# More buffers for the scaled q, k, v sums ahead of the short convolution in a hybrid encoder trunk

## Chip, cores, metric

The kernel runs on one core of one Trainium2 chip, as one launch. The metric is device time in microseconds, the median of several runs. Engines are named as in the profile: PE (TensorE matmuls), DVE (VectorE), ACT (ScalarE), POOL (GpSimd), SP (SyncE, which issues the weight loads).

## What is computed

A two-layer encoder on 256 tokens of width 1024, all in float32. Each layer is half a SwiGLU, a mixer, half a SwiGLU. The mixer has two branches that read one projection `h @ w_in`, and the change lies in the first:

```
gq, gk, gv, gz, gb, ga, c_q, c_kv, k_rope, gate_logits = split_cols(h @ w_in[l])
# branch A, gated DeltaNet
qkv = centred_short_conv(concat([q, k, v]), conv_w)     # depthwise, 5 taps along the sequence, zero edges, then SiLU
qh, kh, vh = l2norm(q), l2norm(k), v                    # 4 heads of 128
o = chunked gated delta rule, forwards + backwards      # decays, a triangular inverse, a state
# branch B, latent attention
q = rmsnorm(c_q) @ w_uq;  kv = rmsnorm(c_kv) @ w_ukv;  softmax attention, 8 heads
y = sigmoid(g_A) * (A @ P_A) + sigmoid(g_B) * (B @ P_B);  x = x + y @ w_out
```

## The kernel before

Every dense product is three matmuls in a reduced float32 format: weights and activations are split into a high and a low part. A weight tile arrives by DMA as `raw`, ACT casts it to `whi` (line 130), DVE subtracts to get `wlo` (line 131), and PE multiplies high by high, low by high and high by low (lines 148 to 150, helper `mm3`). There are three buffers each of `raw`, `whi` and `wlo`, so PE paces the casts, and PE waits whenever a cast or a subtraction comes late.

The tile framework's scheduler decides the order of instructions on each engine from data dependences, buffer reuse and priorities; each engine then works through its own list in order. PSUM sums use the tag `acc` with three buffers.

The mixer takes q, k and v as six groups of 256 channels, `qkv_group(0)` to `(5)`; groups 0 and 1 are q, 2 and 3 are k, 4 and 5 are v. The program calls them in the order 2, 3, 0, 1, then much later 4 and 5. A group is 48 matmuls into one `acc` buffer (line 557), then on DVE: scale by the norm's row `rb` out of PSUM into `pre` (line 565), a first tap into `cv` for each half (line 571), four more taps for each half (line 573), then ACT's tanh into `th` (line 577) and DVE's product into `qkT` or `vT` (line 578). `pre`, `cv` and `th` have one buffer each. POOL writes zeros into the two edge columns at each end of `pre` (lines 563 and 564), which lets every tap read 256 columns.

What stands around it, in the order of the text: the gates' decays (`gdn_decay`: POOL multiplies masks at line 743 and masks the exponentials at line 755, PE sums at line 744), lengths of k (`lengths(4)`: POOL squares `qkT` into a `cv` buffer at line 586, PE sums at 590, DVE turns and reads at 593 and 594, POOL takes the power at 598), the latent of the attention (`latent`, split at lines 115 and 116), the products with `w_ukv` (512 wide) and `w_uq` (384 wide) in `mla_dense(0)`, the z product, coefficients (`nk` at line 714), the chunk matrices `LA` (PE 763, DVE 767), `mla_dense(1)`, two gate products of 512 columns (`gate`, ACT tanh into the tag `gate`, which has six buffers), and the triangular inverse: `gdn_base` copies `LA` into place (ACT 793, DVE 791), POOL runs 30 small steps (lines 805 and 807), DVE and ACT bring the result into `XC` and `ZC` (810 to 816), and PE's first product on it is line 839.

Of the kernel before, what the change touches and what calls it, by code (L numbers as in the profile page):

```python
# [16 lines left out]
ALU = mybir.AluOpType  # L17
# [3 lines left out]
P = 128  # L21
D = 1024
S = 256
# [14 lines left out]
def encoder_trunk(ctx: ExitStack, tc: tile.TileContext, x, positions, norm_ffn1, ffn1_w_gate, ffn1_w_up,  # L38
# [4 lines left out]
    V, A, G, T = nc.vector, nc.scalar, nc.gpsimd, nc.tensor  # L43
# [8 lines left out]
    def acc():  # L52
        return psum.tile([P, 512], F32, tag="acc", name="acc", bufs=3)
# [4 lines left out]
    def gdp():  # L58
        return psum.tile([P, 512], F32, tag="gd", name="gd", bufs=2)
# [59 lines left out]
    def weights(src, nk, w, pool=wpool):  # L119

        raw = wpool.tile([P, 2048], F32, tag="raw", name="raw", bufs=3)
        nc.sync.dma_start(out=raw[:, :nk * w].rearrange("p (k c) -> p k c", c=w),
                          in_=src.rearrange("(k p) c -> p k c", p=P))
        per = 1024 // w
        res = []
        for k0 in range(0, nk, per):
            n = min(per, nk - k0)
            hi = pool.tile([P, 1024], F32R, tag="whi", name="whi", bufs=3)
            lo = pool.tile([P, 1024], F32R, tag="wlo", name="wlo", bufs=3)
            A.copy(out=hi[:, :n * w], in_=raw[:, k0 * w:(k0 + n) * w])  # L130
            V.tensor_tensor(out=lo[:, :n * w], in0=raw[:, k0 * w:(k0 + n) * w], in1=hi[:, :n * w].bitcast(F32),  # L131
                            op=ALU.subtract)
            for k in range(n):
                res.append((hi[:, k * w:(k + 1) * w], lo[:, k * w:(k + 1) * w]))
        return res
# [289 lines left out]
    def mixer(l, next_gain):  # L425
# [7 lines left out]
        with tc.tile_pool(name="mix", bufs=1) as mp:  # L433
            def t2(tag, bufs, shape=(P, NH, P)):
                return mp.tile(list(shape), F32, tag=tag, name=tag, bufs=bufs)
# [17 lines left out]
            rb = mp.tile([P, S], F32, name="rb")  # L453
# [92 lines left out]
            def qkv_group(grp):  # L546

                ps = acc()
                pc = ps.rearrange("p (c s) -> p c s", c=2)
                ws = weights(wl_[:, grp * 256:(grp + 1) * 256], NKC, 256)  # L550

                for c in range(2):
                    cc = slice(c * P, (c + 1) * P)
                    terms = [m for kc, (wh, wlo) in enumerate(ws)
                             for m in ((wh, xh[:, kc]), (wh, xl[:, kc]), (wlo, xh[:, kc]))]
                    for i, (w, a) in enumerate(terms[::-1] if c else terms):
                        T.matmul(pc[:, c].rearrange("p (t s) -> p t s", s=P), lhsT=w[:, cc], rhs=a, start=(i == 0),  # L557
                                 stop=(i == len(terms) - 1))
                if grp >= 4:
                    vT[grp - 4] = ysb[0][:, (grp - 4) * 512:(grp - 3) * 512].rearrange("p (c s) -> p c s", s=S)  # L560
                pre = t2("pre", 1, (P, 2, S + 4))
                cv = t2("cv", 1, (P, 2, S))
                G.memset(pre[:, :, 0:2], 0.0)  # L563
                G.memset(pre[:, :, S + 2:S + 4], 0.0)
                V.tensor_tensor(out=pre[:, :, 2:S + 2], in0=pc, in1=rb[:, None, :].to_broadcast([P, 2, S]), op=ALU.mult)  # L565
                for c in range(2):
                    ch = grp * 2 + c
                    for d in range(5):
                        wc = ccol[:, l * 60 + d * 12 + ch:l * 60 + d * 12 + ch + 1]
                        if d == 0:  # L570
                            V.tensor_scalar(out=cv[:, c], in0=pre[:, c, 0:S], scalar1=wc, scalar2=None, op0=ALU.mult)
                        else:
                            V.scalar_tensor_tensor(out=cv[:, c], in0=pre[:, c, d:d + S], scalar=wc, in1=cv[:, c],  # L573
                                                   op0=ALU.mult, op1=ALU.add)

                th = t2("th", 1, (P, 2, S))
                A.activation(out=th, in_=cv, func=AF.Tanh, scale=0.5)
                V.scalar_tensor_tensor(out=qkT[:, grp * 2:grp * 2 + 2, :] if grp < 4 else vT[grp - 4], in0=th, scalar=1.0,
                                       in1=cv, op0=ALU.add, op1=ALU.mult)

            def lengths(c0):

                pss = gdp()[:, :4 * NT * 32].rearrange("p (c t s) -> p c t s", c=4, t=NT)
                for c in (0, 2):
                    sq = t2("cv", 1, (P, 2, S))
                    G.tensor_tensor(out=sq, in0=qkT[:, c0 + c:c0 + c + 2, :], in1=qkT[:, c0 + c:c0 + c + 2, :], op=ALU.mult)
                    sv = sq.rearrange("p c (t g s) -> p g c t s", t=NT, g=4)
                    for g in range(4):

                        T.matmul(pss[g * 32:(g + 1) * 32, c:c + 2], lhsT=ones, rhs=sv[:, g], start=True, stop=True)  # L590
                rows = t2("rows", 1, (P, 2, 4 * NT * 32))
                A.copy(out=rows[:, 0], in_=pss.rearrange("p c t s -> p (c t s)"))
                V.transpose(out=rows[:, 1], in_=rows[:, 0])
                V.tensor_scalar(out=ssq[:, :, c0:c0 + 4],
                                in0=rows[:, 1].rearrange("p (c t s) -> p t c s", c=4, t=NT)[:, :, :, 0],
                                scalar1=4.0 * EPS, scalar2=None, op0=ALU.add)
                for t in range(NT):
                    G.tensor_tensor(out=rqk[:, t, c0:c0 + 4], in0=ssq[:, t, c0:c0 + 4], in1=neghalf[:, :4], op=ALU.pow)
# [407 lines left out]

            rstd_row()
            qkv_group(2)
            dense(xh, xl, NKC, wl_, C_BA, 400, ev_ba)
            qkv_group(3)  # L1010
            qkv_group(0)
            dense(xh, xl, NKC, wl_, C_KV, 288, ev_kv)
            gdn_scalars()
            gdn_decay(0)
            lengths(4)
            cqT = latent(cq, QL, 0, G_Q + 3 * l)
            qkv_group(1)
# [36 lines left out]
            at1(0)  # L1054
            sts[1] = gdn_first(1)
            lengths(0)
            gdn_second(0, sts[0])
            ga = [gate(C_G)]
# [60 lines left out]
```

## Time and profile before

| | |
|---|---|
| median of 3 runs | 1235.73 us (1235.57 to 1237.52) |
| the profiled execution | 1238.92 us, of which the profile's span is 1237.2 us |
| mean granted TensorE clock | 0.985 of full speed |
| busy | PE 1204.2 us, DVE 770.9 us, ACT 622.4 us, POOL 132.3 us |

Busy time is the sum of an engine's instructions with overlaps counted once. The two layers behave alike: the same lines wait for the same lines twice, some 611 us apart. A wait is put down to the instruction that released it. Times of the trace below are in microseconds from the start of the span, and those of layer 0.

### The profile page before, as it was taken

Reading aid. Unit: us, or ns where it says so; the run is one execution under the profiler, and the core shown is the slowest. Engines: PE = TensorE matmul, PEld = TensorE weight load, DVE = VectorE, ACT = ScalarE, POOL = GpSimd, SP = SyncE. Lnnn points to the kernel's source line nnn. Section 1 sums busy time; section 2 is a strip of 40 time slices with the busy share of each in tenths; the row PEclk is TensorE's granted clock in tenths of the full one; section 3 lists DMA queues with packets and bytes.
Section 4 is the critical chain, followed back from the end, with each engine's and each line's share of the span. In section 5 each row is a group of like instructions: output and inputs, shape, how many; then the busy total and the mean of one; then the engine's idle time right before and its main releaser. Section 6 shows DMA issues by size and latency. Waiting matters only on the chain.

```text
span 1237.2 us, 17605 instructions
## 1 busy us (share of the span) xinstructions
PE 1204.2 (97%) x7064; PEld 1016.9 (82%) x7064; DVE 770.9 (62%) x1125; ACT 622.4 (50%) x911; POOL 132.3 (11%) x238
## 2 busy tenths in 40 slices
PE   9999999899999999999999999997999999999997
PEld 6888889778778888888888888897778888888886
DVE  5665556986857665554555554588858676555554
ACT  6554445547455454444454453465455455544443
POOL 1000001454101000000000000015540000000010
PEclk9999999989899999999999999998998999999999
DMA  7564555445222555556555556553453135565552
GB/s 265 181 197 144 201 188 179 139 125 174 94 88 103 171 185 189 176 173 207 187 178 187 186 170 194 182 158 122 124 168 104 69 138 186 178 198 180 191 187 85
DMA packets 114576, 202.70 MB, mean 164 GB/s; under 512 B 4107, under 2 KB 30399, under 8 KB 114495
## 3 DMA queue, kind: packets, MB, share of 16 engines
q1 hardware_dynamic: 114031, 200.52, 49.9%
q8 instruction: 55, 0.90, 0.3%
q10 hardware_dynamic: 464, 1.06, 0.2%
q14 instruction: 26, 0.21, 0.1%
HBM read 200.52 MB, written 1.05 MB: 163 GB/s over the span
## 4 chain that ended last, share of the span: by engine, by line
PE 87%; DVE 5%; POOL 4%; ACT 2%; issue 2%; DMA 0%; POOLq 0%; SPq 0%; ACTq 0%
PE acc L148 24%; PE acc L149 24%; PE acc L150 24%; PE acc L557 4%; PE ms L198 2%; DVE wlo L131 2%; POOL t L807 1%; PE ms L665 1%; POOL bt L805 1%; PE gd L148 1%; PE gd L149 1%; PE gd L150 1%; PE gd L938 1%; DVE cv L573 1%; PE gd L763 1%
## 5 line engine op out<-in xcount | busy, mean ns | idle before, releaser
L131 DVE TENSOR_TENSOR wlo<-raw,whi 128x1024 fp32r<-128x1024 f32 (+3 forms) x388 | 470.4, 1215 | 368.4 <-ACT whi L130 365.9
L130 ACT CAST whi<-raw 128x1024 fp32r<-128x1024 f32 (+3 forms) x388 | 399.3, 1033 | 424.0 <-PE acc L150 384.1
L149 PE MATMUL acc<-wlo,xh 128*128 128x512 f32 (+3 forms) x968 | 360.6, 374 | 0.0
L150 PE MATMUL acc<-whi,xl 128*128 128x512 f32 (+3 forms) x968 | 357.4, 372 | 0.0
L148 PE MATMUL acc<-whi,xh 128*128 128x512 f32 (+3 forms) x968 | 344.8, 376 | 0.1
L149 PEld LDWEIGHTS acc<-wlo,xh 128*128 128x128 f32 x968 | 182.4, 188 | 29.5 <-issue 0.4
L148 PEld LDWEIGHTS acc<-whi,xh 128*128 128x128 f32 x968 | 181.5, 189 | 30.3 <-ACT xh L115 0.8
L150 PEld LDWEIGHTS acc<-whi,xl 128*128 128x128 f32 x968 | 182.1, 188 | 29.3
L149 PE MATMUL acc<-wlo,hh 128*128 128x512 f32 x352 | 137.4, 390 | 0.0
L150 PE MATMUL acc<-whi,hl 128*128 128x512 f32 x352 | 137.1, 390 | 0.0
L148 PE MATMUL acc<-whi,hh 128*128 128x512 f32 x352 | 127.3, 392 | 0.0
L150 PEld LDWEIGHTS acc<-whi,hl 128*128 128x128 f32 x352 | 66.1, 188 | 13.8
L148 PEld LDWEIGHTS acc<-whi,hh 128*128 128x128 f32 x352 | 66.1, 188 | 13.7
L149 PEld LDWEIGHTS acc<-wlo,hh 128*128 128x128 f32 x352 | 66.1, 188 | 13.3
L148 PE MATMUL acc<-whi,fr 128*128 128x512 f32 (+1 forms) x152 | 60.3, 403 | 9.1 <-DVE pre L565 7.9
L149 PE MATMUL acc<-wlo,fr 128*128 128x512 f32 (+1 forms) x152 | 59.9, 396 | 0.0
L150 PE MATMUL acc<-whi,fr 128*128 128x512 f32 (+1 forms) x152 | 57.5, 395 | 2.4 <-DVE fr L116 2.4
L557 PE MATMUL acc<-xl,whi 128*128 128x256 f32 x192 | 55.3, 288 | 0.0
L557 PE MATMUL acc<-xh,wlo 128*128 128x256 f32 x192 | 54.2, 292 | 1.0 <-DVE wlo L131 1.0
L557 PE MATMUL acc<-xh,whi 128*128 128x256 f32 x192 | 54.9, 289 | 0.0
L573 DVE SCALAR_TENSOR_TENSOR cv<-pre,ccol,cv 128x256 f32<-128x256 f32 x96 | 51.5, 569 | 0.1
L563 POOL MEMSET pre<- 128x4 f32 x12 | 1.2, 104 | 425.3 <-PE acc L150 341.0
(298 smaller groups left out, 1271.9 us busy)
## 6 DMA issues: line engine op xcount, KB each, us to landing
raw<-in_ffn_w_up_dram SPq DMA_DIRECT2D x40, 1024.0 KB, 5.1
raw<-in_ffn_w_down_dram SPq DMA_DIRECT2D x40, 1024.0 KB, 4.9
raw<-in_ffn_w_gate_dram SPq DMA_DIRECT2D x38, 1024.0 KB, 5.0
raw<-in_w_in_dram SPq DMA_DIRECT2D x32, 1024.0 KB, 5.0
raw<-in_w_out_dram SPq DMA_DIRECT2D x8, 1024.0 KB, 4.9
raw<-in_ffn_w_gate_dram SPq DMA_DIRECT2D x12, 512.0 KB, 3.7
raw<-in_ffn_w_up_dram SPq DMA_DIRECT2D x8, 512.0 KB, 3.7
raw<-in_ffn_w_down_dram SPq DMA_DIRECT2D x8, 512.0 KB, 3.3
```

Source lines behind the costliest of these rows:

```text
L130: A.copy(out=hi[:, :n * w], in_=raw[:, k0 * w:(k0 + n) * w])
L131: V.tensor_tensor(out=lo[:, :n * w], in0=raw[:, k0 * w:(k0 + n) * w], in1=hi[:, :n * w].bitcast(F32), op=ALU.subtract)
L148: T.matmul(ps[t][:, :n], lhsT=a1, rhs=w[0], start=start, stop=False)
L149: T.matmul(ps[t][:, :n], lhsT=a1, rhs=w[1], start=False, stop=False)
L150: T.matmul(ps[t][:, :n], lhsT=a2, rhs=w[0], start=False, stop=stop)
L198: T.transpose(out=pt[:, i * S + t * P:i * S + (t + 1) * P], in_=srcs[t][:, (j + i) * P:(j + i + 1) * P], identity=ident)
L557: T.matmul(pc[:, c].rearrange("p (t s) -> p t s", s=P), lhsT=w[:, cc], rhs=a, start=(i == 0), stop=(i == len(terms) - 1))
L573: V.scalar_tensor_tensor(out=cv[:, c], in0=pre[:, c, d:d + S], scalar=wc, in1=cv[:, c], op0=ALU.mult, op1=ALU.add)
L665: T.matmul(sc[:, t * S:(t + 1) * S], lhsT=qT[:, t * P:(t + 1) * P], rhs=kT, start=True, stop=True)
L763: T.matmul(pa[:, (h - hp) * 256:(h - hp + 1) * 256], lhsT=qkT[:, 4 + h, t * P:(t + 1) * P], rhs=qkT[:, h:h + 5:4, t * P:(t + 1) * P], star ...
L805: G.tensor_tensor(out=tv, in0=M[:, b + 1:16, b:b + 1].to_broadcast([P, na, nb]), in1=Y[:, b:b + 1, 0:nb].to_broadcast([P, na, nb]), op=ALU ...
L807: G.tensor_tensor(out=Y[:, b + 1:16, 0:nb], in0=Y[:, b + 1:16, 0:nb], in1=tv, op=ALU.add)
```

## The change

Groups 0 to 3 now scale into a buffer of the tag `gate`, whose six buffers the gates' tanh uses only later; groups 4 and 5 keep `pre` with one buffer. `cv` has two buffers. The scaling instruction (line 565) is emitted under a priority. The tanh is written over the scaled sums, so `th` is gone. The zero edges are gone: the centre tap comes first and writes all 256 columns, and the others touch only the 254 or 255 columns that exist. Lines behind the edit move down by one (573 becomes 574, 577 becomes 578, and so on).

```diff
-                pre = t2("pre", 1, (P, 2, S + 4))
-                cv = t2("cv", 1, (P, 2, S))
-                G.memset(pre[:, :, 0:2], 0.0)
-                G.memset(pre[:, :, S + 2:S + 4], 0.0)
-                V.tensor_tensor(out=pre[:, :, 2:S + 2], in0=pc, in1=rb[:, None, :].to_broadcast([P, 2, S]), op=ALU.mult)
+
+                pre = t2("gate", 6, (P, 2, S)) if grp < 4 else t2("pre", 1, (P, 2, S))
+                cv = t2("cv", 2, (P, 2, S))
+                with tc.high_priority(offset=150):
+                    V.tensor_tensor(out=pre, in0=pc, in1=rb[:, None, :].to_broadcast([P, 2, S]), op=ALU.mult)
                 for c in range(2):
                     ch = grp * 2 + c
-                    for d in range(5):
+                    for d in (2, 0, 1, 3, 4):
                         wc = ccol[:, l * 60 + d * 12 + ch:l * 60 + d * 12 + ch + 1]
-                        if d == 0:
-                            V.tensor_scalar(out=cv[:, c], in0=pre[:, c, 0:S], scalar1=wc, scalar2=None, op0=ALU.mult)
+                        if d == 2:
+                            V.tensor_scalar(out=cv[:, c], in0=pre[:, c], scalar1=wc, scalar2=None, op0=ALU.mult)
                         else:
-                            V.scalar_tensor_tensor(out=cv[:, c], in0=pre[:, c, d:d + S], scalar=wc, in1=cv[:, c],
+                            o, i = (slice(2 - d, S), slice(0, S + d - 2)) if d < 2 else (slice(0, S + 2 - d), slice(d - 2, S))
+                            V.scalar_tensor_tensor(out=cv[:, c, o], in0=pre[:, c, i], scalar=wc, in1=cv[:, c, o],
                                                    op0=ALU.mult, op1=ALU.add)
 
-                th = t2("th", 1, (P, 2, S))
+                th = pre
...
-                    sq = t2("cv", 1, (P, 2, S))
+                    sq = t2("cv", 2, (P, 2, S))
```

The scheduler orders the mixer anew around this. Three places of layer 0 follow; layer 1 has the same order at each of them.

Place one is DVE at the scaling of group 0. Before, its row (line 565) comes when all taps of group 3 are done, and its own taps start three rows later, behind a weight tile:

```order
L573 SCALAR_TENSOR_TENSOR cv<-pre,ccol,cv 128x256
L536 TENSOR_TENSOR glog<-glog,alog 128x16
L131 TENSOR_TENSOR wlo<-raw,whi 128x1024
L565 TENSOR_TENSOR pre<-acc,rb 128x2x256
L578 SCALAR_TENSOR_TENSOR qkT<-th,cv 128x512
L113 TENSOR_TENSOR gl<-glog,gh 128x16
L131 TENSOR_TENSOR wlo<-raw,whi 128x1024
L476 TENSOR_SCALAR krope<-acc,rstd 128x32
L571 TENSOR_SCALAR cv<-pre,ccol 128x256 x2
```

DVE at the same place with the change:

```order
L565 TENSOR_TENSOR gate<-acc,rb 128x512
L574 SCALAR_TENSOR_TENSOR cv<-gate,ccol,cv 128x255
L131 TENSOR_TENSOR wlo<-raw,whi 128x864
L574 SCALAR_TENSOR_TENSOR cv<-gate,ccol,cv 128x255
L535 SCALAR_TENSOR_TENSOR glog<-sa,glog 128x16
L571 TENSOR_SCALAR cv<-gate,ccol 128x256 x2
L574 SCALAR_TENSOR_TENSOR cv<-gate,ccol,cv 128x254
L131 TENSOR_TENSOR wlo<-raw,whi 128x288
```

The scaling stands ahead of the last four taps of group 3, and group 0's first two taps among them; three more of its taps stand ahead of group 3's last product (line 579). Further on, the scaling of group 1 stands ahead of the last product of group 0 and of the 384-wide weight tile, where it stood behind the tile.

Place two is POOL where the decays begin (line 743, `m_le`/`m_ge` are masks, `gh`/`gl` the split log decays). Before:

```order
L743 TENSOR_TENSOR pr<-m_le,gh 128x512
L743 TENSOR_TENSOR pr<-m_le,gl 128x512
L743 TENSOR_TENSOR pr<-m_ge,gh 128x512
L743 TENSOR_TENSOR pr<-m_ge,gl 128x512
L743 TENSOR_TENSOR pr<-m_le,gh 128x512
L107 TENSOR_TENSOR lrs<-rsq,neghalf 128x2
L755 TENSOR_TENSOR g_2087<-g_2087,m_le 128x512
L743 TENSOR_TENSOR pr<-m_le,gl 128x512
L743 TENSOR_TENSOR pr<-m_ge,gh 128x512
L755 TENSOR_TENSOR g_2098<-g_2098,m_ge 128x512
```

POOL there with the change:

```order
L744 TENSOR_TENSOR pr<-m_le,gh 128x512
L587 TENSOR_TENSOR cv<-qkT 128x512
L744 TENSOR_TENSOR pr<-m_le,gl 128x512
L744 TENSOR_TENSOR pr<-m_ge,gh 128x512
L744 TENSOR_TENSOR pr<-m_ge,gl 128x512
L107 TENSOR_TENSOR lrs<-rsq,neghalf 128x2
L744 TENSOR_TENSOR pr<-m_le,gh 128x512
L744 TENSOR_TENSOR pr<-m_le,gl 128x512
L756 TENSOR_TENSOR g_2078<-g_2078,m_le 128x512
```

The first square of `lengths(4)` (line 587) has moved up to second place, with six multiplications by masks queued behind it; it reads the product of group 3 and writes the second `cv` buffer.

Place three is ACT before the first gate product (the second full-width cast of each piece is a weight tile of that product; `m_2728`/`m_2716` are keys of the attention, `m_2727`/`m_2715` its queries). Before:

```order
L629 ACTIVATE m_2728<-acc,lrs 128x4x64
L130 CAST whi<-raw 128x1024
L625 ACTIVATE m_2727<-acc,lrs 128x384
L130 CAST whi<-raw 128x1024
L625 ACTIVATE m_2727<-acc,lrs 128x384
L130 CAST whi<-raw 128x1024
L793 COPY g_2399<-LA_1661 32x8x2x16 x4
```

ACT there with the change:

```order
L630 ACTIVATE m_2716<-acc,lrs 128x4x64
L794 COPY g_2387<-LA_1661 32x8x2x16 x4
L630 ACTIVATE m_2716<-acc,lrs 128x4x64
L130 CAST whi<-raw 128x1024
L794 COPY g_2387<-tb 32x8x2x16
L626 ACTIVATE m_2715<-acc,lrs 128x384
L130 CAST whi<-raw 128x1024
```

The four copies of `LA` have moved from behind the gate product's third cast to ahead of its first.

## Rows read from the trace of the kernel before

**Rows 1.** The page: busy time by engine, and the edge writes.

```profile
PE 1204.2 (97%) x7064; PEld 1016.9 (82%) x7064; DVE 770.9 (62%) x1125; ACT 622.4 (50%) x911; POOL 132.3 (11%) x238
...
L563 POOL MEMSET pre<- 128x4 f32 x12 | 1.2, 104 | 425.3 <-PE acc L150 341.0
```

**Rows 2.** Waits of PE: total us over both layers, times, longest.

```profile
PE acc L148 <- DVE pre L565: 7.9, 2, 3.9
...
PE ms L651 <- ACT qk L654: 2.8, 2, 1.4
```

**Rows 3.** Windows: length, busy us of PE, PEld, DVE, ACT, POOL, granted clock, DMA.

```profile
231.00:247.00 16.00, 10.62 (x70) 8.98 (x69) 16.00 (x22) 6.79 (x16) 13.24 (x12) 0.95 0.42 140
247.00:254.00 7.00, 6.13 (x28) 5.66 (x29) 3.62 (x7) 3.74 (x7) 1.04 (x1) 0.62 0.23 75
...
270.00:275.00 5.00, 3.39 (x12) 2.50 (x12) 5.00 (x13) 4.32 (x9) 0.00 (x1) 0.78 0.12 45
275.00:280.00 5.00, 5.00 (x24) 4.39 (x23) 4.76 (x14) 1.45 (x3) 0.00 (x0) 0.88 0.66 210
...
315.00:320.00 5.00, 2.71 (x74) 2.38 (x74) 3.76 (x11) 3.86 (x9) 0.00 (x0) 0.71 0.01 3
320.00:325.00 5.00, 5.00 (x50) 4.32 (x51) 5.00 (x10) 0.36 (x2) 0.00 (x0) 0.60 0.59 200
```

**Rows 4.** Timeline of DVE, 239 to 248: start, us, instruction, count.

```profile
239.62 3.13 DVE L573 SCALAR_TENSOR_TENSOR cv<-pre,ccol,cv 128x256 f32<-128x256 f32 x3
...
243.85 2.01 DVE L131 TENSOR_TENSOR wlo<-raw,whi 128x768 fp32r<-128x768 f32 x1
245.78 0.87 DVE L573 SCALAR_TENSOR_TENSOR cv<-pre,ccol,cv 128x256 f32<-128x256 f32 x2
246.58 0.55 DVE L131 TENSOR_TENSOR wlo<-raw,whi 128x384 fp32r<-128x384 f32 x1
247.04 0.68 DVE L565 TENSOR_TENSOR pre<-acc,rb 128x512 f32<-128x512 f32 x1
```

**Rows 5.** Timeline of POOL, 243 to 266.

```profile
243.61 1.44 POOL L755 TENSOR_TENSOR g<-g,m_ge 128x512 f32<-128x512 f32 x1
...
248.40 1.04 POOL L586 TENSOR_TENSOR cv<-qkT 128x512 f32<-128x512 f32 x1 [1.55 <-DVE qkT L578]
...
265.07 2.98 POOL L598 TENSOR_TENSOR rqk<-ssq,neghalf 128x4 f32<-128x4 f32 x2
```

**Rows 6.** Timeline of DVE, 253 to 279; in brackets the idle time ahead.

```profile
253.91 1.23 DVE L131 TENSOR_TENSOR wlo<-raw,whi 128x1024 fp32r<-128x1024 f32 x1 [3.38 <-ACT whi L130]
...
268.08 1.25 DVE L714 SCALAR_TENSOR_TENSOR nk<-ssq,rqk 128x8 f32<-128x8 f32 x1 [0.99 <-POOL rqk L598]
...
277.50 1.65 DVE L767 SCALAR_TENSOR_TENSOR LA<-gd,negc,g 128x256 f32<-128x256 f32 x4
```

**Rows 7.** Timeline of ACT, 278 to 287.

```profile
278.77 1.04 ACT L130 CAST whi<-raw 128x1024 fp32r<-128x1024 f32 x1
...
284.24 2.70 ACT L793 COPY g<-LA 32x256 f32<-32x256 f32 x4
```

**Rows 8.** Timeline of PE: the first gate product begins.

```profile
282.19 0.63 PE L148 MATMUL acc<-whi,xh 128*128 128x512 f32 x2
282.65 0.40 PE L149 MATMUL acc<-wlo,xh 128*128 128x512 f32 x1
```

**Rows 9.** Timeline of POOL: the first of 30 steps, lines 805 and 807.

```profile
297.79 0.22 POOL L805 TENSOR_TENSOR bt<-t,t 128x15 f32<-128x15 f32 x1 [9.55 <-DVE t L800]
```

**Rows 10.** Timeline of DVE: what follows the last of these steps.

```profile
312.24 1.18 DVE L810 TENSOR_SCALAR g<-t,half 128x256 f32<-128x256 f32 x2 [6.62 <-POOL t L807]
```

**Rows 11.** Timeline of PE, 306 to 318: the inverse's first product.

```profile
306.06 1.08 PE L692 MATMUL ms<-pr,mv 128*64 128x256 f32 x8
...
310.69 0.40 PE L557 MATMUL acc<-xh,wlo 128*128 128x256 f32 x2
...
317.29 1.07 PE L839 MATMUL gd<-XC,LA 32*32 32x32 f32 x64 [1.71 <-DVE XC L816]
```

## Prediction

> **What bounds the kernel now.** I read the page first. PE is busy 97% of the span, POOL 11% [rows 1]. A gain can come only from the time in which PE stands still or runs at the lower clock, so I went to PE's waits next and then to windows around each of them, all in layer 0; layer 1 repeats them, so a total over two places counts once a layer at half.
>
> Two waits matter for the change [rows 2]. The first is 3.9 us a layer: the `w_uq` product needs the `acc` buffer that the scaling of group 1 (line 565) has to empty. The second is 1.4 us: a transpose at line 651 waits for a copy on ACT that stands behind the tanh of group 1, so again for the convolution. In the stretch ahead of the first wait DVE is busy 16.00 of 16 us, POOL 13.24 and PE only 10.62 [rows 3]. The granted clock falls after each long pause of PE: 0.62 in 247 to 254, 0.78 and 0.88 in the ten microseconds from 270, 0.71 and 0.60 in the ten from 315 [rows 3]. These are mixtures of the two levels, 1.2 and 2.4 GHz. The ten from 270 lose (0.22 + 0.12) x 5 = 1.7 us to it, the ten from 315 (0.29 + 0.40) x 5 = 3.4 us, and the first (1 - 0.62) x 7 = 2.7 us.
>
> DVE is slow in that stretch because POOL runs beside it. Two taps take 0.87 us where POOL has nothing to do, 0.44 each; three take 3.13 us, 1.04 each, at 239.62 beside POOL [rows 4]. A low part of 768 columns takes 2.01 us there [rows 4]; three quarters of the 1.23 us of 1024 columns elsewhere [rows 6] are 0.92. So DVE works at 0.42 to 0.46 of its pace beside POOL.
>
> **The change, part by part.** *Edge writes.* The 24 memsets last 1.2 us together [rows 1], on an engine that idles 89% of the span, ahead of an addition that it isn't late for. I cost them at nothing; if that cover were gone, 1.2 us in all. The taps read 254 or 255 columns instead of 256, under 1% of 0.44 us each: nothing.
>
> *The scaling of group 1* is what the first wait is for. By the order, five of group 0's taps go ahead of the decays' input, the 384-wide low part goes behind the scaling, and everything else ahead of it stays. Before, the 384-wide part occupies DVE from 246.58 to 247.04, 0.46 us, and that goes [rows 4]. The five taps that go forward are 2.2 us; I estimate with DVE's idle share of 38% over the span [rows 1] that 0.8 us of them fills idle time. What POOL costs DVE is 13.24 x (1 - 0.46) = 7.1 us over about nine operations; with the stretch shorter, one of them falls behind the scaling: 0.8 us. The sum is 0.46 + 0.8 + 0.8 = 2.0 us earlier. Bounds: 0.2 us, if POOL's nine operations still all come first, since the square of line 587 is now among them (1.04 us with little beside it) [rows 5]; 3.9 us, the whole wait, if the taps that went forward meet no POOL at all. I take 2.0, near the middle.
>
> Rows show DVE and POOL taking turns here. The Trainium skill, page "SBUF — State Buffer", section "Who interferes with whom", says more: a DVE instruction with two SBUF inputs and a GpSimd instruction that reads SBUF share a port pair, and the one that holds it blocks the other for its whole length. That speaks against the change, because a square moves into the fullest stretch: by that rule the gain at this place would be the lower bound. The durations of rows 4, at 0.42 to 0.46 rather than one operation at a time in full, lie near it but don't decide it, since each engine's queue also matters.
>
> *The way to `nk`* (line 714). It waits for POOL's two powers, 2.98 us from 265.07, and then is itself slowed by POOL to end at 268.08 + 1.25 = 269.33 [rows 5, 6]. DVE idles 3.38 us ahead of 253.91 [rows 6], and group 1's taps now fill that time: eight of 0.44 us, 3.5 us. POOL's first square, 1.04 us at 248.40 [rows 5], is moved out of the way, but a mask operation like the 1.44 us at 243.61 slips into this stretch in its place. `nk` then comes earlier by between 1.0 us (the square) and 2.0 us (the head start): I take 1.6, so its end is 267.7. The tanh of group 1 comes some microseconds earlier too, so the 1.4 us wait at line 651 and the low clock of 1.7 us behind it should be gone. Nothing else is queued to take the place of that wait up to 276.
>
> *The first gate product* is where I expect the gain to stop. From `nk`'s end to the end of the four `LA` products, 277.50 + 1.65 = 279.15, pass 9.8 us [rows 6]; one product of 0.6 us (line 578, now ahead) leaves it, 9.2 us, so `LA` is ready at 276.9. But ACT's four copies of `LA`, 2.70 us, which stood behind the third cast of the gate product at 284.24 [rows 7], now stand ahead of its first. With a scaling of 256 columns between, about 0.4 us (a cast of 1024 columns takes 1.04), that is 276.9 + 2.7 + 0.4 + 1.04 = 281.0 [rows 7], and the low part is there some 1.2 us later (a low part's 1.23 us of rows 6), at about 282.15. Before, the first low product starts at 282.65 [rows 8]. All that was won ahead, 2.0 + 1.4 + part of the clock, has shrunk to **0.5 us**. PE is ready at about 278 and stands there 3 to 4 us, a pause of the length that went before the low clock at 247 to 254 [rows 2, 3]. A new low stretch like the 1.7 us at 270 is the nearest row; I take 1.2, since PE does some work in between. Bounds: nothing and 2.7 us (rows 3's first).
>
> *The inverse.* POOL's chain of 30 steps starts at 297.79 and ends as DVE's next row starts, at 312.24: 14.4 us [rows 9, 10]. By the order, the three DVE instructions ahead of it stand one weight tile earlier. A tile of 1024 columns is 24 products, 5.00 us at 0.88 [rows 3], 4.4 us at the full clock; I take 4.2, so the chain starts at 293.6 and ends at 308.0. From there the result needs DVE's 1.18 us of rows 10, two transposes of 512 and 256 columns (by the 0.68 us that the scaling of 512 columns takes in rows 4, about 1.0 us) and one low part of 1.23 us that stands between them: 3.2 us with what overlaps, where before 5.1 us pass to 317.29 [rows 10, 11] with other work between. `XC` is there at 311.2. PE, however, also wants it sooner: line 839's products stood behind 56 products of group 4 and stand now behind 13. At 0.40 - 0.28 = 0.12 us each [rows 11] PE gets there at 306.06 + 1.08 + 13 x 0.12 = 308.7, so the wait is about 2.5 us, as before (0.5 + 1.7 + 0.6, of which rows 11 have the 1.7). If the 5.1 us stay, the wait is 4.4 us. The clock's loss behind it is 3.4 us in rows 3; as the rest of group 4 is now left to do at once, I take a quarter of it back, 0.9 us, bounds 1.7 us back and 1.9 us more wait.
>
> **The sum.** A layer gains 0.5 us to the gate product, loses 1.2 us of clock there, gains 0.9 us at the inverse: 0.2 us. Bounds: the wait and low clock that don't come add 2.7 us; a longer wait at the inverse, or a full 2.7 us of low clock, takes 2 to 3 us. Both layers go the same way: 0.4 us in 1238.92, with 4 to 6 us either side. The profiled execution lies 3.2 us above the median, which I put down to no part of the kernel, and take the difference from the median: 1235.73 - 0.4 = **1235.3 us**.
>
> **Rivals.** *Faster:* the gate's casts are not late, because `LA` comes out sooner than I sum, with POOL done sooner. Then the waits of 3.9 and 1.4 us and the low clock behind them (2.7 and 1.7) go: 9.7 us a layer, 19.4 in all, 1216 us if whole. Half of it, the likelier case, gives 1226 us. For it speaks that DVE's 3.38 us of idle time and POOL's after 249 lie right behind the full stretch; against it, that the copies are ahead of the cast for certain and wait for all of `LA`.
>
> *Slower:* the same place, the other way. DVE gets `LA` out later than 277.4, the point from which the low part comes after 282.65. Every microsecond later is one of PE's in each layer, and the 1.7 to 2.7 us of low clock come on top. If contention takes 2 us there, 1.5 + 2 = 3.5 us a layer, 1243 us. For it speaks rows 4's 0.42 and the square in the full stretch; against it, POOL's lighter load behind.
>
> *Nothing moves:* the scaling waits for the same DVE work whatever its buffer, and DVE's and POOL's total work is unchanged. The order speaks against it; its time is 1235.7 and its chance is within that of the forecast.
>
> **How the numbers follow.** About 0.2%, 2.5 us, is what a measurement of this kernel can tell from no change. I give the forecast within that bound 0.36, the faster rival 0.34, the slower 0.30. The range takes in the half-sized faster case and the slower one with a microsecond more a layer: 1224 to 1245 us. The forecast's own range is 1233 to 1238.
>
> **What would show it.** Right: the 3.9 us wait for line 565 shrinks to about 2; the 1.4 us one at line 652 (651 now) is gone and the clock in 270 to 276 is full; a new PE wait of about 3 us for the first cast of the gate product, which itself waits for line 794, and a clock below 1 behind it; DVE's idle time after 247 is filled; the wait for `XC` stays at 2 to 3 us with fewer group 4 products ahead. Wrong: no wait at the gate product (faster), the first gate low product later than 282.65 (slower), or a wait at a place that I don't name.

## The result: faster by 0.5%

The changed kernel takes 1230.5 us (median of 5 runs, 1230.0 to 1232.5) where the kernel before, timed beside it, takes 1237.52 us (median of 5). The ratio is 0.9947, with a 95% interval of 0.9931 to 0.9963. The time lies in the forecast range, but not in the case that was held likeliest: the forecast was no measurable change, and 0.5% is one that can be measured.

The profiled execution has a span of 1228.3 us, 8.9 less than before. In both profiles the ACT row of line 262 marks the last gate of the first half SwiGLU and the first of the second, so what lies between them is the mixer. Timeline of ACT, after:

```profile
129.66 0.48 ACT L262 ACTIVATE sil<-acc,rstd 128x256 f32<-128x256 f32 x1 [0.39 <-PE acc L150]
445.86 1.27 ACT L262 ACTIVATE sil<-acc,rstd 128x512 f32<-128x512 f32 x2
735.78 0.48 ACT L262 ACTIVATE sil<-acc,rstd 128x256 f32<-128x256 f32 x1 [0.39 <-PE acc L150]
1052.49 1.27 ACT L262 ACTIVATE sil<-acc,rstd 128x512 f32<-128x512 f32 x2
```

The same rows of before:

```profile
129.55 0.48 ACT L262 ACTIVATE sil<-acc,rstd 128x256 f32<-128x256 f32 x1 [0.39 <-PE acc L150]
450.65 1.27 ACT L262 ACTIVATE sil<-acc,rstd 128x512 f32<-128x512 f32 x2
...
740.54 0.48 ACT L262 ACTIVATE sil<-acc,rstd 128x256 f32<-128x256 f32 x1 [0.39 <-PE acc L150]
...
1061.61 1.27 ACT L262 ACTIVATE sil<-acc,rstd 128x512 f32<-128x512 f32 x2
```

With the change 316.2 us lie between the first row and the second and 316.7 between the third and the fourth; before, 321.1 us twice. All of the gain lies in the two mixers, 4.9 and 4.4 us in these two profiles.

PE's waits of layer 0 from 224 to 335 us after the change (total us, times, longest) answer to [rows 2]:

```profile
PE acc L148 <- ACT whi L130: 2.3, 1, 2.3
PE acc L150 <- DVE fr L116: 2.0, 2, 1.7
PE gd L840 <- DVE XC L817: 1.3, 1, 1.3
```

The 3.9 us wait for the scaling and the 1.4 us wait at the transpose are gone. A new one of 2.3 us stands at the first cast of the gate product. The windows answer to [rows 3] (columns as there):

```profile
231.00:247.00 16.00, 13.08 (x85) 10.78 (x83) 16.00 (x22) 8.99 (x19) 12.97 (x10) 0.95 0.48 160
247.00:254.00 7.00, 7.00 (x40) 5.75 (x37) 7.00 (x10) 3.99 (x7) 7.00 (x9) 0.88 0.22 75
...
270.00:275.00 5.00, 5.00 (x26) 4.51 (x25) 5.00 (x12) 0.79 (x2) 0.00 (x0) 1.00 0.37 108
275.00:280.00 5.00, 2.28 (x11) 1.60 (x9) 3.23 (x7) 4.94 (x9) 0.00 (x0) 0.94 0.26 102
280.00:285.00 5.00, 5.00 (x17) 3.99 (x17) 4.56 (x7) 4.62 (x9) 3.81 (x6) 0.72 0.42 115
...
305.00:310.00 5.00, 3.72 (x87) 2.90 (x86) 3.68 (x6) 2.81 (x5) 1.21 (x3) 1.00 0.15 19
310.00:315.00 5.00, 4.29 (x150) 3.87 (x149) 3.28 (x8) 2.40 (x8) 0.00 (x0) 1.00 0.53 194
315.00:320.00 5.00, 5.00 (x125) 4.72 (x126) 3.92 (x9) 2.95 (x8) 0.78 (x2) 1.00 0.01 3
```

DVE's idle time after 247 is filled (7.00 of 7.00). The clock is full at 270 to 275, low behind the new wait (0.94, 0.72), and full behind the inverse's first product, where it had fallen to 0.60 before. The rows on the path, one engine after the other; timeline of DVE, answering to [rows 4, 6, 10]:

```profile
243.84 0.67 DVE L565 TENSOR_TENSOR gate<-acc,rb 128x512 f32<-128x512 f32 x1
...
264.14 1.26 DVE L715 SCALAR_TENSOR_TENSOR nk<-ssq,rqk 128x8 f32<-128x8 f32 x1 [0.83 <-POOL rqk L599]
...
305.23 1.19 DVE L811 TENSOR_SCALAR g<-t,half 128x256 f32<-128x256 f32 x2 [3.94 <-POOL t L808]
```

Timeline of ACT, answering to [rows 7]:

```profile
274.68 2.61 ACT L794 COPY g<-LA 32x256 f32<-32x256 f32 x4 [4.00 <-DVE LA L768]
...
277.69 1.03 ACT L130 CAST whi<-raw 128x1024 fp32r<-128x1024 f32 x1
```

Timeline of PE, answering to [rows 8, 11]:

```profile
278.78 0.50 PE L148 MATMUL acc<-whi,xh 128*128 128x512 f32 x1 [2.33 <-ACT whi L130]
...
280.26 0.63 PE L149 MATMUL acc<-wlo,xh 128*128 128x512 f32 x1
...
308.67 0.75 PE L840 MATMUL gd<-XC,LA 32*32 32x32 f32 x64 [1.28 <-DVE XC L817]
```

Timeline of POOL, answering to [rows 9], and ahead of it what POOL runs up to the scaling of group 1, answering to [rows 5]:

```profile
231.01 1.08 POOL L744 TENSOR_TENSOR pr<-m_le,gh 128x512 fp32r<-128x512 f32 x1 [14.49 <-ACT gh L112]
233.05 2.04 POOL L587 TENSOR_TENSOR cv<-qkT 128x512 f32<-128x512 f32 x1 [0.96 <-DVE gl L113]
...
241.49 1.22 POOL L744 TENSOR_TENSOR pr<-m_le,gl 128x512 fp32r<-128x512 f32 x1
244.67 1.66 POOL L756 TENSOR_TENSOR g<-g,m_le 128x512 f32<-128x512 f32 x1 [1.96 <-DVE cs L750]
...
290.73 0.22 POOL L806 TENSOR_TENSOR bt<-t,t 128x15 f32<-128x15 f32 x1 [4.00 <-DVE t L801]
```

Eight operations of POOL stand from 231.01 to the one at 241.49; the next waits for DVE behind the scaling. Before, ten ran in the stretch.

### The profile page after: what moved, and what is told of

Same layout as the page of the kernel before. It is cut to its first block, busy times and chain, and to the rows that moved or that the text cites. A ratio compares the mean times of both kernels' runs of the same rounds, so it can differ in the third digit from the quotient of the medians.

```text
span 1228.3 us, 17567 instructions
## 1 busy us (share of the span) xinstructions
PE 1197.6 (98%) x7064; PEld 1010.1 (82%) x7064; DVE 775.1 (63%) x1125; ACT 623.5 (51%) x911; POOL 135.4 (11%) x214
## 4 chain that ended last, share of the span: by engine, by line
PE 82%; DVE 10%; POOL 2%; issue 2%; ACT 2%; DMA 0%; POOLq 0%; SPq 0%; ACTq 0%; DVEq 0%
PE acc L148 23%; PE acc L149 23%; PE acc L150 23%; DVE wlo L131 3%; PE acc L557 3%; DVE cv L574 2%; PE ms L198 2%; POOL t L808 1%; POOL bt L806 1%; DVE LA L768 1%; ACT whi L130 1%; PE ms L666 1%; PE gd L149 1%; PE gd L148 1%; PE gd L150 1%
## 5 line engine op out<-in xcount | busy, mean ns | idle before, releaser
L262 ACT ACTIVATE sil<-acc,rstd 128x512 f32<-128x512 f32 (+1 forms) x48 | 31.0, 654 | 29.6 <-PE acc L150 29.5
L834 POOL MEMSET Z<- 128x1024 f32 x4 | 3.7, 959 | 341.1 <-PE acc L150 341.1
```

The costliest lines, as they stand in the source:

```text
L262: A.activation(out=sil[t][:, :w], in_=ps, func=AF.Silu, scale=rstds[0][:, t:t + 1])
```

## The experiments

Each kernel was timed in five rounds beside the kernel before. That kernel's own runs spread: beside the last experiment 17 of them lie from 1234.99 to 1240.49 us. So ratios to before are compared, the change's being 0.9947.

**Parts of the change.** First the taps without edges alone, on the kernel before.

```diff
-                pre = t2("pre", 1, (P, 2, S + 4))
+                pre = t2("pre", 1, (P, 2, S))
                 cv = t2("cv", 1, (P, 2, S))
-                G.memset(pre[:, :, 0:2], 0.0)
-                G.memset(pre[:, :, S + 2:S + 4], 0.0)
...
```

> Only the taps without zero edges; one place each for the scaled sums, the sums of taps and the tanh, no priority. Queue theory (the gain comes from the scaling of the next group standing ahead of taps and of group 3's product, which needs the places): nothing is gained, 1236 us within 0.2%, PE still waits about 3.9 us a layer for the scaling of group 1 and 2.8 us before the inverse. Rival (shorter taps and 24 writes fewer on POOL thin out the turns that DVE and POOL take): half of the gain or more, 1233 us or less, and that wait under 2.5 us.

1235.58 us, ratio 0.999 (0.9981 to 0.9999). PE's waits, whole run:

```profile
PE acc L148 <- DVE pre L564: 7.9, 2, 3.9
...
PE ms L651 <- ACT qk L654: 2.8, 2, 1.4
```

These two are [rows 2] again to the tenth. The edges are worth some 0.1%, by the interval 0.2% at most; the rival falls. Next, the changed kernel without the priority.

```diff
-                with tc.high_priority(offset=150):
-                    V.tensor_tensor(out=pre, in0=pc, in1=rb[:, None, :].to_broadcast([P, 2, S]), op=ALU.mult)
+                V.tensor_tensor(out=pre, in0=pc, in1=rb[:, None, :].to_broadcast([P, 2, S]), op=ALU.mult)
```

> The changed kernel without the priority of the scaling. By the order the scaling of group 1 stands where it does with priority; only rows ahead of it differ. Queue theory: the places do the work, 1230.5 us within 0.2%. Rival (the priority does it): 1234 us or more, and a wait for the scaling of group 1 of over 2 us comes back.

1229.69 us, 0.9936 (0.9922 to 0.9949): the intervals of both overlap, so nothing shows that the priority is worth anything. The scaling of group 1 starts at 243.72. Next, one buffer for all scaled sums.

```diff
-                pre = t2("gate", 6, (P, 2, S)) if grp < 4 else t2("pre", 1, (P, 2, S))
+                pre = t2("pre", 1, (P, 2, S))
```

> The changed kernel, but all groups scale into the one buffer pre; two cv buffers and the priority stay. By the order the scaling of group 1 stands behind group 0's product again and behind the 384-wide low part, but the coefficients and LA come as early as with the change. Queue theory by places: the wait of the first kind is back, 3 to 4 us a layer, but the inverse stays early: about half of the gain, 1232 to 1235 us. Rival (all of the gain hangs on the scaling): 1236 us or more.

1232.81 us, 0.9962 (0.9949 to 0.9974), some 70% of the gain. The wait for the scaling is longer than before, 5.9 us, but PE hardly stands before the inverse (it stands 1.4 us two microseconds behind it, at line 683). Waits of layer 0, 224 to 335 us:

```profile
PE acc L148 <- DVE pre L565: 5.9, 1, 5.9
...
PE gd L840 <- DVE XC L817: 0.3, 1, 0.3
```

So the wait that I put first in the profile can get worse while the kernel gets faster: most of the gain comes without the places for the scaled sums. What this run keeps is the second `cv`, the taps without edges, the priority and the tanh written over the sums; the last of these no run takes out alone. Next, one `cv` buffer.

```diff
-                cv = t2("cv", 2, (P, 2, S))
+                cv = t2("cv", 1, (P, 2, S))
...
-                    sq = t2("cv", 2, (P, 2, S))
+                    sq = t2("cv", 1, (P, 2, S))
```

> The changed kernel with one cv buffer: the scaling may go ahead, the taps behind it may not. By the order group 1's taps stand behind four weight tiles again and nk comes later. Queue theory: the 3.9 us wait is gone, the 1.4 us wait at the transpose and the late LA are back: 1232 to 1236 us. Rival (the scaling alone is what counts): 1230.5 us within 0.2%.

1244.65 us, 1.0061 (1.0049 to 1.0074): slower than before, which neither theory had. The scaling is early (243.20), and PE waits elsewhere; whole run:

```profile
PE ms L493 <- DVE g L974: 9.1, 4, 4.0
PE gd L840 <- DVE XC L817: 6.1, 2, 3.1
PE ms L683 <- DVE pr L678: 4.2, 4, 1.8
```

With one `cv` the taps of a group wait until the sums of the group before are used up, the scheduler orders the rest of the mixer otherwise, and PE stands 3.1 us a layer before the inverse's first product and up to 4.0 us for the branch's output (line 974 is in `gdn_out`). The early scaling without the second `cv` is no gain; with it, it is one.

**The copies of `LA` on ACT.** The changed kernel with the four copies ahead of the first gate cast on POOL:

```diff
-                        A.copy(out=W[r].rearrange("p i (s n) -> p n s i", s=2)[:, d * N8:(d + 1) * N8],
+                        (A.copy if d else G.tensor_copy)(out=W[r].rearrange("p i (s n) -> p n s i", s=2)[:, d * N8:(d + 1) * N8],
```

> The changed kernel with the four copies of LA (line 794, ahead of the first gate cast) on POOL, which is idle there. Theory of the step on ACT: the wait of 2.3 us a layer for that cast shrinks to under 0.5 us and the clock of 0.72 in 280 to 285 (with 0.94 before it: 1.7 us) goes up: 2 to 4 us a layer, 1223 to 1227 us, as long as POOL's copies aren't needed before the inverse starts. Rival (the cast is late for DVE, its copy and scaling of queries, or the weight's transfer): the wait stays within 0.5 us and the time at 1230.5.

1226.59 us, 0.9903 (0.9887 to 0.992). The first low product of the gate starts at 277.95 and not at 280.26, and PE's wait of 2.3 us for the cast is gone; one of 0.6 us for a scaling on ACT is left. With the clock behind it 3.8 us a layer were to be had (2.3 of wait and 1.5 of clock); the mixers are 2.0 and 1.7 us shorter (314.2 and 315.0 by the marker). The windows show why only half comes out in this profile: the clock stays up at 280 to 285, and falls instead behind a longer stand for `XC`, 2.0 us.

```profile
275.00:280.00 5.00, 4.05 (x19) 2.99 (x18) 4.90 (x8) 4.12 (x7) 4.79 (x7) 1.00 0.25 99
280.00:285.00 5.00, 5.00 (x24) 4.14 (x23) 4.87 (x8) 3.62 (x7) 3.56 (x5) 1.00 0.66 209
...
305.00:310.00 5.00, 3.97 (x75) 3.55 (x76) 3.45 (x6) 3.37 (x7) 0.00 (x0) 0.66 0.65 208
```

The step of the prediction on ACT's order holds: the copies ahead of the cast make PE wait, and they last about what was said (2.61 us for 2.70).

**POOL beside DVE.** The squares of `lengths(4)` on ACT:

```diff
-                    G.tensor_tensor(out=sq, in0=qkT[:, c0 + c:c0 + c + 2, :], in1=qkT[:, c0 + c:c0 + c + 2, :], op=ALU.mult)
+                    A.activation(out=sq, in_=qkT[:, c0 + c:c0 + c + 2, :], func=AF.Square)
```

> The changed kernel with the two squares of lengths(4) on ACT and not on POOL. Theory of turns (each POOL operation beside DVE costs DVE about 0.8 us): the scaling of group 1 comes 0.5 to 1 us earlier and nk 1 to 2 us earlier, worth 1 to 2 us a layer: 1227 to 1229 us. Rival (POOL's squares fit beside DVE's work and cost nothing, or ACT's casts come later for them): 1230.5 us within 0.2% or slower.

1227.21 us, 0.9907 (0.9891 to 0.9924): faster than the change, by about what was expected, and only in part for the reason expected. The mixer of layer 0 starts 1.25 us later in this profile (the marker stands at 130.91 and not at 129.66), so times are compared from there. The scaling of group 1, at 246.53, comes 1.4 us later than with the change, against the theory; `nk` ends at 265.12, 1.5 us earlier, as the theory had it. POOL is no less busy in 231 to 247 than with the change (13.45 us for 12.97), since the mask operations move up into the room. PE's largest wait of layer 0 is now another:

```profile
PE acc L148 <- DVE mv L631: 3.2, 2, 2.7
...
```

The mixers are 0.3 and 2.1 us shorter than with the change. How the 3 us divide is not settled by this run. Both moves together:

> Both moves together: the squares on ACT, the four copies of LA on POOL. If the two theories hold and add up: 1221 to 1226 us. Rival (what is won ahead waits again at the gate product or at the inverse's result): no better than the better one of the two alone.

1223.89 us, 0.9882 (0.9863 to 0.9901), below both single moves and the fastest kernel here, 1.2% below before. Without the priority as well:

> Squares on ACT and LA's copies on POOL (as in the run of both) and no priority for the scaling. If the priority is worth nothing, as alone: 1223.9 us within 0.2%. Rival (with ACT's queue fuller the priority matters): 1226 us or more.

1224.97 us, 0.9907 (0.9893 to 0.9921). The intervals overlap; nothing shows that the priority matters here either.

**The inverse.** Its first product was to go behind all of group 4, with POOL's chain as early as with the change:

```diff
-            with tc.high_priority(offset=2000):
+            with tc.high_priority(offset=-1500):
                 inv0(0)
```

> The changed kernel with the inverse's first product (line 840) at a lower priority: by the order it stands behind all of group 4's products again, as before the change, while POOL's chain starts as early as with the change; everything up to there is the same. Theory (the early result is worth the short wait for XC and the clock that doesn't fall): the wait of 1.3 us at line 840 is gone in both layers, so 1228 us if nothing behind it is late. Rival (what hangs on the inverse is then late by the 5 us of group 4's 43 products, and PE waits further on, at the second half of the inverse or at the copies of DVE): 1230.5 us or more.

1259.94 us, 1.0184 (1.0163 to 1.0204): the rival's side, and by far more than it said. But the edit did more than was meant. Line 840 starts at 316.57, 7.9 us later than with the change and without a wait, yet its first 64 products, one block in both other kernels, now come in eight pieces between other products, until 341.8. Timeline of PE, this run:

```profile
316.57 0.31 PE L840 MATMUL gd<-XC,LA 32*32 32x32 f32 x10
...
341.53 0.25 PE L840 MATMUL gd<-XC,LA 32*32 32x32 f32 x4
```

ACT's copy of their result, which the inverse's second product reads, comes 31.6 us later. Timeline of ACT, the changed kernel and then this run:

```profile
310.63 0.38 ACT L842 COPY t<-gd 128x256 f32<-128x256 f32 x1
```

```profile
342.21 0.38 ACT L842 COPY t<-gd 128x256 f32<-128x256 f32 x1
```

In the kernel before, whose order this run was to bring back, that copy stands at 319.99. The mixer ends 15.6 us later (461.50 for 445.86 in the marker above). One window of the changed kernel, then of this run:

```profile
340.00:440.00 100.00, 98.82 (x567) 82.09 (x566) 66.79 (x118) 51.89 (x97) 5.42 (x6) 1.00 0.38 124
```

```profile
340.00:440.00 100.00, 90.06 (x863) 72.37 (x862) 58.65 (x111) 44.03 (x89) 5.85 (x8) 0.95 0.28 96
```

PE stands 9.9 us of these 100 where it stands 1.2 with the change. What hangs on the inverse is a chain that PE's other work doesn't cover when it comes 32 us late. What a delay of 8 us alone would cost, and so whether PE's short stand at line 840 pays for its early place, this run does not show. With the same priority on both moves:

> Squares on ACT, LA's copies on POOL, and the inverse's first product at a lower priority. With both moves the wait for XC was 0.45 us a layer, so there is 0.9 us to win at most: 1223 us if nothing behind is late. Rival (PE waits further on instead): 1225 us or more.

1256.66 us, 1.0167 (1.015 to 1.0184): a like loss, and the copy of line 842 is as late (340.02). Next, a longer chain on POOL:

```diff
+                for o_ in (ALU.subtract, ALU.add) * 2:
+                    G.tensor_tensor(out=Y, in0=Y, in1=eye16, op=o_)
```

> The changed kernel with four more operations on POOL behind the inverse's 30 steps (subtract and add the identity twice, which leaves the values), 128x256 each, some 2.5 us together; by the order line 840's products then stand about ten of group 4's products later, 1.2 us, so XC is late for PE by about 1.3 us more: a wait of 2.5 us as in the kernel before. Theory (a longer stand of PE at this place brings the low clock back, as before the change): 1.3 us of wait and about 1.7 to 3.4 us of clock a layer, 1236 to 1240 us, and a granted clock of 0.6 to 0.8 in the ten microseconds behind line 840. Rival (the clock there has nothing to do with the length of the stand): only the wait, 1232 to 1234 us, clock 1.00.

1233.7 us, 0.9976 (0.9965 to 0.9987), about half of the gain lost. PE stands 1.8 us where it stood 1.3, and in this profile the clock is lower behind it:

```profile
310.00:315.00 5.00, 3.20 (x83) 2.96 (x82) 4.47 (x9) 1.81 (x4) 0.70 (x2) 0.93 0.00 0
315.00:320.00 5.00, 4.68 (x125) 4.33 (x125) 3.89 (x7) 2.91 (x7) 0.00 (x0) 0.73 0.16 21
```

The clock leans to the theory, the time lies in the rival's range; the stand grew by 0.5 us and not by 1.3. That the longer stand is what lowers the clock is not shown: the next run stands 1.7 us at this place with a clock of 1.00 behind it. Last, the kernel before with only the copies of `LA` on POOL (the edit of the run above): by the order nothing changes ahead of the gate product's third cast.

> The kernel before the change with only the four copies of LA on POOL: by the order nothing differs up to there (the waits of 3.9 and 1.4 us stay), and the inverse starts sooner, by the 2.7 us of the copies or by a weight tile. Theory (about 3 us a layer of the change's gain lie at the inverse: a shorter stand for XC and the clock behind it): the stand before the inverse's first product under 2 us, the clock behind it above 0.8, 2 to 3 us a layer: 1230 to 1233 us where before has 1236. Rival (the gain lies all ahead of the gate product): the time of before within 0.2%, with PE standing elsewhere instead.

1233.83 us, 0.9976 (0.9963 to 0.9988): 0.8 us above the theory's range, and the interval takes in the rival's 0.2%. The waits of 3.9 and 1.4 us are still there, POOL's chain ends 2.9 us earlier (DVE's row at 309.30), PE's stand for `XC` is 1.7 us as before, and the clock stays up behind it:

```profile
310.00:315.00 5.00, 3.34 (x87) 3.10 (x86) 4.05 (x8) 2.25 (x6) 0.33 (x1) 1.00 0.01 3
315.00:320.00 5.00, 4.86 (x154) 4.32 (x153) 4.30 (x9) 2.77 (x6) 0.00 (x0) 1.00 0.19 47
```

The moved copies, and with them an earlier inverse, give 0.24% without the change, nearly half of what the change gives. How much of it is the earlier inverse and how much the clock of this place, the run doesn't separate.

## Why the prediction was right in part, step by step

| step, layer 0 | forecast | measured |
|---|---|---|
| scaling of group 1 earlier | 2.0 us | 247.04 - 243.84 = 3.2 us |
| end of `nk` earlier | 1.6 us | 269.33 - 265.40 = 3.9 us |
| `LA` ready for ACT | 276.9 | 274.68 |
| first low product of the gate earlier | 0.5 us | 282.65 - 280.26 = 2.4 us |
| clock lost behind the new wait | 1.2 us | 0.06 x 2.28 + 0.28 x 5.00 = 1.5 us |
| POOL's chain | 293.6, 14.4 us | 290.73, 14.5 us |
| from its end to line 840 | 3.2 us | 3.4 us |
| stand at line 840 | 2.5 us | 1.3 us |
| clock won back behind it | 0.9 us | 0.29 x 2.71 + 0.40 x 5.00 = 2.8 us |

The clock rows here count the low clock while PE was busy; the prediction counted the whole windows, which made its prices of the low clock too high (3.4 us where PE's busy time gives 2.8). The mechanisms were the ones that the runs show: both old waits go, ACT's copies of `LA` make a new one at the gate product with a low clock behind it in this profile, and PE asks sooner for the inverse and waits for it. The size was not: 0.2 us a layer were forecast, and the time lies in the range because the range was made to hold the rivals too. Two terms of the sum were too small.

**The term that failed first is the scaling's, "one of them falls behind the scaling: 0.8 us".** Two of POOL's operations fell behind it (eight ahead and not ten), since the exponentials' masking waits for a copy on DVE that now stands behind the scaling. With twice 0.8 the step's own sum is 0.46 + 0.8 + 1.6 = 2.9 us. The second part of the same fault is `nk`: I bounded it by a head start of 2.0 us. The head start was 3.2, and `nk` ends 3.9 us earlier because POOL's two powers, for which it waits, end at 264.11 and not at 268.05. So 2.4 us and not 0.5 arrive at the gate product. The lower bound of 0.2 us, which the Trainium skill's rule (page "SBUF — State Buffer", section "Who interferes with whom") gave at this place, did not come: the rule itself agrees with rows here (below), but it says what happens to one operation, not how many stand ahead.

**One term came out by luck, the 9.2 us from `nk` to `LA`** (measured 274.68 - 265.40 = 9.3). The four products at 277.50 that I took for the last of `LA` were not. Four more follow in the kernel before, of which ACT's copies need two, and they wait for PE's last products of line 763. Timelines of DVE and of PE, before, then of PE, after:

```profile
281.52 1.66 DVE L767 SCALAR_TENSOR_TENSOR LA<-gd,negc,g 128x256 f32<-128x256 f32 x4 [0.45 <-PE gd L763]
```

```profile
280.45 1.02 PE L763 MATMUL gd<-qkT 128*128 128x256 f32 x4
```

```profile
270.01 1.03 PE L764 MATMUL gd<-qkT 128*128 128x256 f32 x4
```

With the change PE runs these products 10.4 us sooner, and POOL's chain starts 7.1 us earlier and not 4.2 as forecast.

**The second term that was too small is at the inverse: "I take a quarter of it back, 0.9 us".** All of it came back in the profile, 2.8 us, and the stands there shrank from 0.5 + 1.7 + 0.6 to 1.3 + 0.7 us. How the clock divides between this place and the gate product is not the kernel's own: the run without priority, as fast, loses nothing at the gate product and 0.10 x 3.35 + 0.24 x 5.00 = 1.5 us here. Both places together give back 1.3 us in either profile, where -1.2 + 0.9 = -0.3 was forecast. The run of the kernel before with the copies on POOL makes it likely that this place carries a gain; why the clock comes back here stays open.

From measured terms a layer gains 2.4 - 1.5 + 0.8 + 2.8 = 4.5 us; the mixers gained 4.9 and 4.4. The medians, 7.0 us apart, give 3.5 a layer. The likely reason for the difference is the profiled execution of before, which lies above its median. The run without edges has the same order of waits and nearly the time of before. Its clock is 1.00 in 270 to 280 where [rows 3] have 0.78 and 0.88, and its mixers last 319.1 and 318.9 us, so that the change's are 2.9 and 2.2 us shorter. I took a loss of 1.7 us a layer at 270 as the kernel's, and it is that of some executions.

The measured time lies between the forecast, 1235.3 us, and the faster rival's half-sized case, 1226 us. Of that rival's grounds one came, `LA` sooner than I summed; its condition, that the gate's casts are not late, did not, since PE waits 2.3 us for the first. The slower rival's condition, the low part later than 282.65, was far off at 280.26. That nothing moves is refuted by the scaling, which comes 3.2 us earlier, and by the time. What stays open is where the run with the squares on ACT wins its time, which of the reorderings makes the run with one `cv` slow, and what the early place of the inverse's first product is worth by itself.

## What to carry to other kernels

A stand of PE is not priced by its length alone: ask what the chain behind it carries, because a kernel that waited 5.9 us for its largest wait beat one that waited 3.9, and one that took away a 1.3 us wait, and made the chain behind it 32 us late, lost 29 us. When a buffer is added ahead of a chain, add the one that the next step writes too; the scaling's places without the second `cv` made this kernel slower, and the second `cv` without the places kept some 70% of the gain. Before a loss is put down to a moved instruction, look where all of it went: a lower priority scattered one block of products over 25 us. And when two engines share a stretch, count how many of the other's operations stand ahead of the row that is waited for, not only how long one of them is.

## What the runs showed of the hardware

**The clock does not fall behind every stand.** The run without priority stands 2.34 us at the same gate product as the changed kernel, which stands 2.33. Its windows:

```profile
275.00:280.00 5.00, 2.27 (x11) 1.55 (x9) 3.27 (x7) 4.94 (x9) 0.00 (x0) 1.00 0.29 113
280.00:285.00 5.00, 5.00 (x23) 4.06 (x23) 4.51 (x8) 4.93 (x10) 3.75 (x6) 1.00 0.41 109
```

The changed kernel has 0.94 and 0.72 there. At the inverse's first product three kernels stand for 1.7 us: the clock behind it is 0.71 and 0.60 in the kernel before (where two stands of 0.5 and 0.6 us lie around it), 0.90 and 0.76 without priority, and 1.00 when only the copies of `LA` move. A single profile's low clock is therefore no constant of a kernel. The spread of before goes with it: of its executions beside the experiments, those from 1239.1 us up show a mean granted clock of 0.984 or 0.985, those up to 1236.33 us one of 0.988 to 0.991.

**A tiny operation on DVE waits for all of POOL's.** Timeline of DVE in the changed kernel, a 128x2 operation with one input, while POOL multiplies masks:

```profile
238.46 1.00 DVE L106 TENSOR_SCALAR rsq<-lss 128x2 f32<-128x2 f32 x1
```

It ends at 239.46, as POOL's 2.02 us from 237.41 end at 239.43. Before, where POOL had nothing to do, the same row takes 0.16 us at 239.09. And a row with an input from PSUM is not held up: line 476 (`krope<-acc,rstd`) takes 0.24 us in both kernels in the midst of POOL's masks. Both agree with the Trainium skill, page "SBUF — State Buffer", section "Who interferes with whom": an operation of this kind can take the port pair that DVE shares with GpSimd, and whoever holds the pair blocks the other for a whole instruction; an instruction with at most one input in SBUF and outside such modes does not contend.

**POOL's copies cost more than ACT's.** The four copies of `LA` take 2.61 us on ACT and 3.79 us on POOL in the run that moved them (4.54 in the kernel before with them on POOL), and still pay: POOL had stood idle for 9.33 us ahead of them in the first of these runs and 11.58 us in the second.
